# Where the next expert weights are put: ten places of four kinds of tiles instead of five of one kind, and two of four gathers spread over two pairs

## The chip, the cores and the metric

The kernel runs on one core of a Trainium2 chip. The metric is device time in microseconds (us) of one execution; the median of several runs is quoted, and one further execution is recorded by the hardware profiler. Inside a core, TensorE (PE in the rows) multiplies, VectorE (DVE), ScalarE (ACT) and GpSimd (POOL) do the element-wise work, and SyncE (SP) issues most of the copies from device memory. Each engine works through its own list of instructions in order; they wait for each other by semaphores. Copies issued by SP run on 16 DMA engines.

## The reference

The model has two layers of one kind and then two of another, over 512 tokens of width 1024. The change touches only the mixture of experts of the first kind: 16 experts, each with three 1024 x 1024 float32 matrices, and each expert takes the 64 tokens that score highest for it.

```python
def expert_choice_moe(h, w_router, w_gate_e, w_up_e, w_down_e):
    cap = EC_CAPACITY * s // N_EXPERTS                      # 64 tokens
    affinity = jax.nn.softmax((h @ w_router).astype(jnp.float32), axis=-1)
    top_aff, idx = lax.top_k(jnp.swapaxes(affinity, 1, 2), cap)
    xe = h[bidx, idx]
    hid = jax.nn.silu(jnp.einsum('becd,edf->becf', xe, w_gate_e)) * jnp.einsum('becd,edf->becf', xe, w_up_e)
    ye = jnp.einsum('becf,efd->becd', hid, w_down_e)
    return jnp.zeros_like(h).at[bidx, idx].add(ye * top_aff[..., None].astype(ye.dtype))
...
        x = x + expert_choice_moe(rms_norm(x, g_moe[i]), w_router[i], w_exp_gate[i], w_exp_up[i], w_exp_down[i])
        ple_gate = jax.nn.sigmoid(rms_norm(x, g_ple[i]) @ w_ple_gate[i])
        x = x + ple_gate * (p[i] @ w_ple[i])
```

## The kernel before

The experts are worked through in **eight pairs** (`for pr in range(8)` in `moe`). The two experts of a pair use the two halves of the PE's columns (`two[fh][j * 64:...]`, j = 0 and 1), so that a multiplication of the one can run beside a multiplication of the other. A pair is twelve **steps**: four for gate, four for up, four for down. A step uses two **loads** of 1 MB, one of each expert: 2 x 128 rows of 1024 float32 (`take()`), and consists of eight multiplications. So a pair has 24 loads, a layer 192.

`load()` issues the next load on SP's queue and takes its place from a pool of tiles. `plan` says from which:

- `wst`: five tiles of 1 MB (`NW = 5`), which stage all other weights of the kernel too;
- `pt`: three tiles of 1 MB, two of which hold the one-hot matrices `oh` of the slots during the pairs;
- `fm`: tiles of 256 KB, 24 of them; a load takes four, in four copies;
- `wh`: the pair of tiles `wh`, `wl` of 512 KB, two of each; a load takes one of each, in two copies;
- `tr` and `ae`: two more kinds, used once a layer.

A tile that is used again is loaded when the last multiplication that reads its old contents is done; since SP issues in order, a load that waits for its place holds up all later loads. Before, the list `PLAN` uses the further kinds for the first 25 loads of a layer; from there on (`plan.pop(0) if plan else "wst"`) all go to the five `wst` places.

Between the steps of a pair stands other work of the PE, one piece a step, taken from the list `side` by `step()`: the **scatter** of the pair before (`sct`, eight pieces of two multiplications, added to `x` by DVE), `turned` (one-hots of the pair turned, `oht` and `asl`) and, in pairs 1, 3 and 5, the **gather** of the tokens of the next four experts (`xe`, four pieces of 16 multiplications). When `side` is empty, `step()` takes a piece of `late`, the work that prepares the next stage: `turn` (`pps`), eight products `pw` of six multiplications each, whose weights `wple` are loaded and split into `wh`, `wl` first, and the loading (`wpg`) and splitting of the next gate's first weights. Within a pair, the result of gate and up goes through ACT (`sg`), DVE (`hd`), PE (`hdt`) and ACT or DVE (`ht`) before down can begin.

The order on each engine is not that of the program text alone: a scheduler interleaves the instructions, and may put a multiplication of one expert before its partner's weights are expected, as rows below show.

Of the kernel before, what the change touches and what calls it, by code (L numbers as in the profile page):

```python
# [16 lines left out]
S = 512  # L17
D = 1024
KT = 8
NB = 4  # L20
P = 128
# [11 lines left out]
PLAN = ["pt"] * 2 + ["wst"] * 5 + ["fm"] * 3 + ["wh"] * 2 + ["tr", "ae"] + ["pt"] + ["wst"] * 5 + ["fm"] * 3 + ["wh"] * 2  # L33
# [52 lines left out]
class Net:  # L86
# [12 lines left out]
    def claim(self, *tiles):  # L99
        """first touch, so that a tile has its place before those first used from here on"""  # L100
        for t in tiles:
            self.nc.gpsimd.memset(t[:, :1], 0.0)
# [60 lines left out]

    def wtile(self, w, segs, kts):
        """w: AP [K, N]; segs: column ranges; kts: K-tiles -> SBUF view [P, len(kts), cols]"""
# [12 lines left out]
    def wsplit(self, parts, k, m):  # L178
        """parts: list of (dst column 0.., source AP [P, k', m'...]) -> hi, lo [P, k, m]"""
# [23 lines left out]
    def ahead(self, n):  # L203
        """what is traced inside comes up to n instructions earlier in the scheduler's order"""
        return self.tc.high_priority(offset=n) if n else nullcontext()

    def proj_fm(self, w, c0, c1, xh, xl, evac, kn=KT, rope=False, early=0, pre=()):
        """feature-major: out[c, t] for columns c0..c1 (<= 256 a unit); evac(i, m, psum[m, S])"""
# [27 lines left out]
    def proj_tm(self, w, segs, xh, xl, evac):  # L236
        """token-major: out[t, cols] in runs of 256 columns; evac(i, tb, psum[P, 256])"""
# [17 lines left out]
    def split(self, out_h, out_l, src, scale=None):  # L255
        """exact two-part split of src (PSUM or SBUF) into float32r hi, lo"""
# [8 lines left out]

    def inv_rms(self, ms, n):
        """ms: [P, n] SBUF mean square + eps -> ms ** -0.5"""
        r = self.sm("rr", n)
        self.nc.gpsimd.tensor_tensor(r, ms, self.mhalf[:, :n], op=OP.pow)  # L269
        return r  # L270

    def rows(self, r, width=None):
        """r: [P tok, NB] per-token column(s) -> PSUM [P, S], the value of each token on all partitions"""
# [9 lines left out]
    def mean_sq(self, gains=(None,), on=None):  # L283
        """for each gain the mean of (x g)^2 of the residual's tokens, PSUM [P, NB] each"""
# [21 lines left out]
    def rms_cols(self, on=None):  # L306
        """rsqrt(mean(x^2)+eps) of the residual's tokens, [P, NB]"""
# [7 lines left out]
    def norm(self, g, shift=None, before=None):  # L315
        """before: gain of a norm that x has still to go through first (self.r1: its tokens' factors)"""
# [30 lines left out]
    def norm_raw(self, g):  # L347
        """x * g in two parts; the norm's factor of each token is left to the products' ends"""
# [7 lines left out]
    def factors(self, on=None):  # L356
        """the norm's factor of each token: self.rt [P tok, NB] and self.rb [P, S], the same on all partitions"""
# [6 lines left out]
    def fmul(self, out, ps, scale=None, m=P):  # L364
        """feature-major product times the tokens' factors (and a constant)"""
# [5 lines left out]
    def tmul(self, out, ps, tb):  # L371
        """token-major product times the tokens' factors"""
# [7 lines left out]

    def setup(self):
# [7 lines left out]
        # x to feature-major  # L389
# [18 lines left out]
        # vectors, feature-major: column j of vec is row j of the stacked [rows, 128]  # L408
# [30 lines left out]
    def t5_bias(self):  # L439
        """T5 bias vector of each head over the relative position"""  # L440
# [47 lines left out]
    def sgu(self, l, xh, xl, w_in, vv):  # L488
        """spatial gating; vv: gelu(v) token-major tiles (cols 256:512 of each)"""
# [49 lines left out]
    def probs(self, e, s, dst, qb, nk):  # L539
        """normalise e by 1/s [P,1], transpose into dst[:, kt, qb*P:]"""  # L540
# [12 lines left out]
    def gqa(self, l, qkv, av):  # L553
        nc, ap = self.nc, self.ap
        # gains folded into the rope tables, six heads wide
# [83 lines left out]
    def diff_pre(self, l, xh, xl, w_in):  # L639
        nc = self.nc  # L640
        # q and k of a map in exact parts, stacked: (qh qh ql) . (kh kl kh)
# [19 lines left out]
    def diff(self, l, cv, stacked):  # L661
        nc, ap = self.nc, self.ap
        lam_init = 0.8 - 0.6 * math.exp(-0.3 * l)
        # lambda
# [69 lines left out]
    def dt_mul(self, l, w_in):  # L734
        """four partial products of the time steps, on 32 partitions each, from x itself"""
# [15 lines left out]
    def ssm(self, l, xh, xl, w_in, dtv, ahead):  # L751
# [31 lines left out]
        # cumulative sums within each chunk: acs (inclusive towards l) and what is left to the end  # L783
# [11 lines left out]
        # conv + silu, feature-major: x0 x1 b0 b1 c0 c1  # L795
# [17 lines left out]
        # token-major x and b  # L813
# [16 lines left out]
        for g in range(2):  # L830
            # scores [s, (c l)]
# [29 lines left out]
            # inside the chunk  # L861
# [8 lines left out]
            # across chunks: the states before each, [n, (hh p)]  # L870
# [101 lines left out]
    def add_out(self, w, macc, scale, gate=None, fills=(), before=None):  # L972
        """x += gate * ((scale * macc) @ w); before: see norm"""
# [21 lines left out]
    def mix1(self, l, fills):  # L995
        """fills: pieces of work that hang on nothing here"""
# [43 lines left out]
    def moe(self, l, fill, late):  # L1040
        """fill, late: pieces of work that hang on nothing here, for the time of the routing and for after it"""
        nc, ap = self.nc, self.ap
        # the experts' weights in the order of their use, two K-tiles of one expert at a time
# [32 lines left out]
        # the first go wherever there is room during the routing  # L1076
        plan = PLAN[:]
        for _ in range(PLAN.index("tr")):
            load()
        gm = self.vec["g_moe"][:, l * 8:l * 8 + 8]  # L1080
# [5 lines left out]
        # router on x itself; the norm's factor of each token follows on the logits  # L1086
# [34 lines left out]
        # normed x (without its gain) token-major in two exact parts  # L1121
# [19 lines left out]
        # one-hot of the slot of each token in each expert, two tiles of eight experts  # L1141
# [9 lines left out]
        def gather(g4, d2, xs):  # L1151
            # tokens of four experts, feature-major
# [9 lines left out]
            t = self.fm("xe")  # L1162
# [9 lines left out]
        def turned(pr, out):  # L1172
            # slot-major one-hot and affinities of the pair
# [23 lines left out]
        def step():  # L1197
            if side:
                side.pop(0)()
            elif late and pr:  # L1200
                late.pop(0)()
        xs, nxt = [], []
        onehot(0)
        for pr in range(8):
            tn = []
            if pr in (1, 3, 5):
                onehot(pr // 2 + 1)
            side.append(lambda pr=pr, tn=tn: turned(pr, tn))
            if pr % 2 and pr < 7:
# [528 lines left out]
```

## Time and profile before

| | us |
|---|---|
| median of 3 runs (3690.09 to 3692.62) | 3691.54 |
| the profiled execution, span from first to last instruction | 3690.2 |
| eight pairs of the first layer (557.9 to 1131.5) | 573.6 |
| eight pairs of the second layer (1721.4 to 2300.7) | 579.3 |
| mean granted clock of the PE, of full speed | 0.984 |

The profiled execution is reported by its span alone. A row of a stretch gives: its begin and end, its length, and for PE, PEld (the PE's loading of stationary operands), DVE, ACT and POOL the busy time and in brackets the instructions; then the granted clock, the busy share of the DMA engines and the GB/s that they moved. The stretches of the pairs begin at the first expert multiplication of each pair (192 matmul records a pair, two for each multiplication). A row of a timeline gives begin, duration, engine, line, operation, what is written from what, shape and count, and in square brackets how long the engine had been idle before and what ended that. Matmul rows end about 0.07 us after the next one has begun, since matmuls are pipelined.

### The profile page before, as it was taken

The numbers are of one execution on the slowest core, as the hardware profiler recorded it, in microseconds if no ns is written. First come the engines' busy times: TensorE is split into PE (matmuls) and PEld (weight loads), VectorE is DVE, ScalarE is ACT, GpSimd is POOL, SyncE is SP. The second block draws the span as 40 slices with busy tenths as digits, with TensorE's granted clock in tenths as the row PEclk, the third lists the DMA queues.
The fourth block names the chain that finished last, engine by engine and source line by source line (L and its number), as shares of the span: only waits on it lengthen the run. The fifth ranks groups of instructions, "written<-read, shape, count | busy, mean of one in ns | idle before, by whom it ended". The sixth has DMA issues, their size and how long they took to land. (4 is left out here: it accounts for less than half of the span.)

```text
span 3690.2 us, 41806 instructions
## 1 busy us (share of the span) xinstructions
PE 3505.6 (95%) x15959; PEld 2302.9 (62%) x15959; DVE 1804.6 (49%) x3532; ACT 1134.1 (31%) x2209; POOL 416.9 (11%) x630
## 2 busy tenths in 40 slices
PE   8999989999999999999999899899999999999998
PEld 7867774333336877776333333676768877676887
DVE  7667651111106776773111011787564458866344
ACT  4334731000004443462000001424443332444333
POOL 0110620000000110061000000131030003203000
PEclk9999999999999999999999999999999999999999
DMA  5223758888896132565888989222213333220322
GB/s 171 90 69 111 225 203 311 327 330 330 312 358 207 58 106 82 169 224 214 320 329 315 357 311 359 89 77 85 69 35 107 99 107 100 64 81 31 114 96 69
DMA packets 335580, 655.93 MB, mean 178 GB/s; under 512 B 28188, under 2 KB 205680, under 8 KB 335380
## 3 DMA queue, kind: packets, MB, share of 16 engines
q1 hardware_dynamic: 312128, 628.77, 47.8%
q0 software_dynamic: 8192, 15.22, 1.8%
q10 hardware_dynamic: 15059, 9.28, 0.8%
q8 instruction: 126, 2.06, 0.2%
q14 instruction: 75, 0.61, 0.1%
HBM read 629.59 MB, written 14.70 MB: 175 GB/s over the span
## 5 line engine op out<-in xcount | busy, mean ns | idle before, releaser
L150 PE MATMUL pj<-xh,wh 128*128 128x512 f32 x1808 | 729.0, 404 | 15.0 <-DVE gb L147 6.6
L150 PE MATMUL pj<-xh,wl 128*128 128x512 f32 (+1 forms) x1808 | 725.7, 402 | 10.9 <-DVE wl L139 10.9
L150 PE MATMUL pj<-xl,wh 128*128 128x512 f32 (+1 forms) x1808 | 726.0, 402 | 0.9 <-DVE xl L147 0.7
L150 PE MATMUL eg<-wst,xe 128*64 128x512 f32 x1872 | 535.3, 604 | 47.8 <-DMA wst<-in_w_exp_up_dram 40.2
L129 ACT ACTIVATE wh<-wst 128x1024 fp32r<-128x1024 f32 (+2 forms) x368 | 339.0, 930 | 758.1 <-PE pj L150 565.1
L139 DVE TENSOR_TENSOR wl<-wst,wh 128x1024 fp32r<-128x1024 f32 (+2 forms) x368 | 412.2, 1123 | 310.9 <-ACT wh L129 310.4
L150 PEld LDWEIGHTS pj<-xh,wh 128*128 128x128 f32 x1808 | 342.8, 190 | 110.8 <-DVE gb L147 9.8
L150 PEld LDWEIGHTS pj<-xh,wl 128*128 128x128 f32 (+1 forms) x1808 | 342.6, 190 | 103.3 <-DVE wl L139 14.2
L150 PEld LDWEIGHTS pj<-xl,wh 128*128 128x128 f32 (+1 forms) x1808 | 342.5, 189 | 94.1 <-issue 12.8
L150 PEld LDWEIGHTS eg<-wst,xe 128*64 128x64 f32 x1872 | 167.7, 136 | 367.8 <-issue 249.2
L150 PE MATMUL ey<-wst,ht 128*64 128x512 f32 x960 | 298.7, 602 | 14.4 <-DVE ht L136 6.3
L139 DVE TENSOR_TENSOR hd<-sg,eg 128x512 f32<-128x512 f32 x32 | 21.9, 685 | 451.9 <-PE eg L150 422.9
L150 PEld LDWEIGHTS ey<-wst,ht 128*64 128x64 f32 x960 | 87.3, 136 | 161.2 <-issue 132.8
L269 POOL TENSOR_TENSOR rr<-msb,mhalf 128x4 f32<-128x4 f32 x9 | 9.2, 1021 | 1518.8 <-DVE msb L143 1518.8
L150 PE MATMUL pt<-wh,xh 128*128 128x256 f32 x512 | 145.8, 285 | 1.5 <-DVE ro L139 1.2
L150 PE MATMUL pt<-wl,xh 128*128 128x256 f32 x512 | 144.7, 283 | 0.0
L150 PE MATMUL pt<-wh,xl 128*128 128x256 f32 x512 | 144.7, 283 | 0.0
L139 DVE TENSOR_TENSOR x<-x,sct 128x512 f32<-128x512 f32 x128 | 82.3, 682 | 118.6 <-PE sct L150 118.6
L129 ACT ACTIVATE e<-e,nm 128x512 f32<-128x512 f32 (+3 forms) x192 | 111.2, 581 | 69.7 <-DVE nm L143 69.2
L129 ACT ACTIVATE sg<-eg 128x512 f32<-128x512 f32 x32 | 19.1, 596 | 323.1 <-PE eg L150 323.1
L1364 POOL TENSOR_TENSOR wada<-wada 128x1024 f32<-128x1024 f32 (+1 forms) x48 | 101.8, 2121 | 133.0 <-ACT wada L129 131.2
L134 ACT ACTIVATE ht<-hdt 128x512 f32<-128x512 f32 x16 | 9.6, 597 | 342.6 <-PE hdt L154 342.6
(485 smaller groups left out, 5380.7 us busy)
## 6 DMA issues: line engine op xcount, KB each, us to landing
wst<-in_w_exp_gate_dram SPq DMA_DIRECT2D x120, 1024.0 KB, 5.0
wst<-in_w_exp_down_dram SPq DMA_DIRECT2D x120, 1024.0 KB, 7.4
wst<-in_w_exp_up_dram SPq DMA_DIRECT2D x114, 1024.0 KB, 7.4
wst<-in_w_in_dram SPq DMA_DIRECT2D x90, 1024.0 KB, 5.4
wst<-in_w_branch_gate_dram SPq DMA_DIRECT2D x32, 1024.0 KB, 5.8
wada<-in_w_ada_dram SPq DMA_DIRECT2D x24, 1024.0 KB, 5.3
wst<-in_w_out_dram SPq DMA_DIRECT2D x16, 1024.0 KB, 7.7
xd<-x SPq DMA_DIRECT2D x32, 256.0 KB, 2.1
```

Source lines behind the costliest of these rows:

```text
L129: return self.nc.scalar.activation(out, in_, func, **kw)
L134: self.nc.scalar.activation(out, in_, AF.Copy)
L139: return self.nc.vector.tensor_tensor(out, a, b, op=op)
L150: return self.nc.tensor.matmul(out, lhsT, rhs, start=start, stop=stop, **kw)
L269: self.nc.gpsimd.tensor_tensor(r, ms, self.mhalf[:, :n], op=OP.pow)
L1364: nc.gpsimd.tensor_tensor(t[:, :k], t[:, :k], t[:, k:2 * k], op=OP.add)
```

## The change

`PLAN` is replaced by a list `FIRST` of 11 loads for the time of the routing (12 before), followed by one each in `tr` and `ae` as before, and then a `RING` of ten places, repeated until 144 loads, those of pairs 0 to 5, are planned: one `pt`, five `wst`, two of four `fm` tiles, two `wh`/`wl`. The loads of pairs 6 and 7 go to `wst` alone. The gathered tokens no longer take new `fm` tiles in each gather, but two fixed sets of four (`xes`), claimed by eight small writes on POOL. `GATHER` says which pair does which pieces: group 1 wholly in pair 1 as before, group 2 half in pair 2 and half in pair 3 (before: pair 3), group 3 half in pair 4 and half in pair 5 (before: pair 5). The pieces of `late` come only from pair 6 on, and then one a step beside a piece of `side` (`if late and pr >= 6` instead of `elif late and pr`).

```diff
-PLAN = ["pt"] * 2 + ["wst"] * 5 + ["fm"] * 3 + ["wh"] * 2 + ["tr", "ae"] + ["pt"] + ["wst"] * 5 + ["fm"] * 3 + ["wh"] * 2
+FIRST = ["pt"] * 2 + ["wst"] * 5 + ["fm"] * 2 + ["wh"] * 2
+RING = ["pt"] + ["wst"] * 5 + ["fm"] * 2 + ["wh"] * 2
+GATHER = {1: (1, (0, 1, 2, 3)), 2: (2, (0, 1)), 3: (2, (2, 3)), 4: (3, (0, 1)), 5: (3, (2, 3))}
...
-        plan = PLAN[:]
-        for _ in range(PLAN.index("tr")):
+        plan = FIRST + ["tr", "ae"]
+        while len(plan) < 6 * 24:
+            plan += RING
+        plan = plan[:6 * 24]
+        for _ in FIRST:
             load()
+        xes = [[self.fm("xe") for _ in range(4)] for _ in range(2)]
+        self.claim(*xes[0], *xes[1])
...
-            t = self.fm("xe")
+            t = xes[g4 % 2][d2]
...
             if side:
                 side.pop(0)()
-            elif late and pr:
+            if late and pr >= 6:
                 late.pop(0)()
...
-            if pr in (1, 3, 5):
-                onehot(pr // 2 + 1)
-            side.append(lambda pr=pr, tn=tn: turned(pr, tn))
-            if pr % 2 and pr < 7:
+            g4, part = GATHER.get(pr, (0, ()))
+            if part and part[0] == 0:
+                onehot(g4)
                 nxt = []
-                for d2 in range(4):
-                    side.append(lambda g4=pr // 2 + 1, d2=d2, nx=nxt: gather(g4, d2, nx))
+            side.append(lambda pr=pr, tn=tn: turned(pr, tn))
+            for d2 in part:
+                side.append(lambda g4=g4, d2=d2, nx=nxt: gather(g4, d2, nx))
```

**SP, the loads of pairs 1 and 2.** Each row is a copy into the tile named first, with its shape and how many stand in a row; `we` are the tiles of the further kinds. Before:

```order
L1069 DMA wst<-in_w_exp_gate_dram 128x2x1024 x7
L1069 DMA wst<-in_w_exp_up_dram 128x2x1024 x8
L1069 DMA wst<-in_w_exp_down_dram 128x2x1024 x8
L1069 DMA wst<-in_w_exp_gate_dram 128x2x1024 x8
L1069 DMA wst<-in_w_exp_up_dram 128x2x1024 x8
```

Now, from the first gate loads of pair 1 on:

```order
L1071 DMA wst<-in_w_exp_gate_dram 128x2x1024 x5
L1059 DMA we<-in_w_exp_gate_dram 128x512 x8
L1064 DMA wewh<-in_w_exp_gate_dram 128x1024
L1064 DMA wewl<-in_w_exp_gate_dram 128x1024
L1064 DMA wewh<-in_w_exp_up_dram 128x1024
L1064 DMA wewl<-in_w_exp_up_dram 128x1024
L1071 DMA we<-in_w_exp_up_dram 128x2x1024
L1071 DMA wst<-in_w_exp_up_dram 128x2x1024 x5
```

Ten loads that were ten copies of 1 MB are now six of 1 MB, eight of 256 KB and four of 512 KB. In the program each of these loads waits for the step that used the load ten before it; before, for the step that used the load five before it.

**ACT, pairs 2 and 3.** ACT evacuates half of each gather piece (`xe`) and each product (`pw`), so its list shows in which pair they stand; `yh` begins the scatter of the pair. Before:

```order
L129 ACTIVATE oht<-oht 128x512
L129 ACTIVATE ph_5718<-pps 128x512
L129 ACTIVATE ph_5727<-pps 128x512
L129 ACTIVATE pw_5761<-pw 128x512
L129 ACTIVATE pw_5782<-pw 128x512
L129 ACTIVATE yh<-ey_5677,asl 128x512
L129 ACTIVATE yh<-ey_5678,asl 128x512
L129 ACTIVATE sg<-eg_5796 128x512
L134 ACTIVATE ht<-hdt 128x512
L129 ACTIVATE sg<-eg_5797 128x512
L129 ACTIVATE oht<-oht 128x512
L129 ACTIVATE xe<-xe,vec_158 128x256 x4
```

Now:

```order
L131 ACTIVATE oht<-oht 128x512
L131 ACTIVATE xe<-xe,vec_158 128x256 x2
L131 ACTIVATE yh<-ey_5741,asl 128x512
L131 ACTIVATE yh<-ey_5742,asl 128x512
L131 ACTIVATE sg<-eg_5866 128x512
L136 ACTIVATE ht<-hdt 128x512
L131 ACTIVATE sg<-eg_5867 128x512
L131 ACTIVATE oht<-oht 128x512
L131 ACTIVATE xe<-xe,vec_158 128x256 x2
```

The four pieces of gather 2 stood in pair 3 and now stand two and two; the work on `pps` and `pw` has left pair 2.

**PE, the beginning of pair 6.** `eg` are the expert multiplications of gate, written for one half of the result each. Before:

```order
L150 MATMUL eg_6672<-wst,xe 64x512
L150 MATMUL eg_6673<-wst,xe 64x512
L150 MATMUL sct<-oht,yh 128x512
L150 MATMUL sct<-oht,yl 128x512
L150 MATMUL sct<-oht,yh 128x512
L150 MATMUL sct<-oht,yl 128x512
L150 MATMUL sct<-oht,yh 128x512
L150 MATMUL eg_6672<-wst,xe 64x512
L150 MATMUL eg_6673<-wst,xe 64x512
L150 MATMUL eg_6672<-wst,xe 64x512 x2
L150 MATMUL eg_6673<-wst,xe 64x512 x2
```

Now, from its third step on:

```order
L152 MATMUL pw<-ph_6797,wh 128x512
L152 MATMUL pw<-pl_6798,wh 128x512
L152 MATMUL sct<-oht,yh 128x512
L152 MATMUL sct<-oht,yl 128x512
L152 MATMUL pw<-ph_6797,wl 128x512
L152 MATMUL pw<-ph_6806,wh 128x512
L152 MATMUL pw<-pl_6807,wh 128x512
L152 MATMUL pw<-ph_6806,wl 128x512
L152 MATMUL eg_6779<-wst,xe 64x512
L152 MATMUL eg_6780<-wst,xe 64x512
```

All eight products `pw` stand in pair 6 now (before: two in pair 2, three each in pairs 4 and 6). In both kernels, two multiplications of the same step often stand alone ahead of another piece, as the first two rows of before: they read the weights of one expert, and their partners come after the piece.

## Rows read from the trace of the kernel before

**Rows 1.** The page: span and busy time of the PE.
```profile
span 3690.2 us, 41806 instructions
...
PE 3505.6 (95%) x15959; PEld 2302.9 (62%) x15959; DVE 1804.6 (49%) x3532; ACT 1134.1 (31%) x2209; POOL 416.9 (11%) x630
```
**Rows 2.** Stretches: pairs 0 to 7 of layer 0, in columns as above.
```profile
557.90:610.00 52.10, 51.39 (x256) 26.02 (x258) 6.51 (x16) 6.34 (x11) 0.00 (x0) 1.00 0.88 331
610.00:685.10 75.10, 73.08 (x299) 29.97 (x295) 14.55 (x23) 7.86 (x13) 0.00 (x0) 1.00 0.81 304
685.10:756.60 71.50, 66.74 (x249) 25.06 (x248) 10.15 (x18) 5.93 (x10) 0.00 (x0) 1.00 0.87 338
756.60:836.10 79.50, 74.50 (x294) 30.41 (x293) 10.94 (x20) 5.56 (x10) 0.00 (x0) 1.00 0.86 330
836.10:909.00 72.90, 67.83 (x248) 25.28 (x247) 8.94 (x16) 5.45 (x9) 0.00 (x0) 1.00 0.85 332
909.00:989.70 80.70, 74.71 (x294) 30.45 (x293) 10.83 (x20) 5.55 (x10) 0.00 (x0) 1.00 0.84 325
989.70:1062.80 73.10, 67.34 (x247) 25.41 (x246) 8.89 (x16) 5.45 (x9) 0.31 (x1) 0.98 0.86 331
1062.80:1131.50 68.70, 61.14 (x226) 21.65 (x225) 10.10 (x17) 4.97 (x7) 0.00 (x0) 1.00 0.98 375
sum 573.60, PE 536.73 PEld 214.25 DVE 80.90 ACT 47.11 POOL 0.31; mean PE 67.09 PEld 26.78 DVE 10.11 ACT 5.89 POOL 0.04
```
**Rows 3.** Stretches: the sum over the eight pairs of layer 1.
```profile
sum 579.30, PE 538.30 PEld 213.23 DVE 80.25 ACT 48.02 POOL 0.00; mean PE 67.29 PEld 26.65 DVE 10.03 ACT 6.00 POOL 0.00
```
**Rows 4.** SP's queue, pairs of layer 0: waited for what, total us, times, longest.
```profile
SPq L1069 <- PE eg L150: 298.8, 110, 11.4
SPq L1069 <- PE ey L150: 176.6, 46, 8.0
```
**Rows 5.** Short stretches inside pairs 3 and 6 of layer 0, same columns.
```profile
776.60:804.60 28.00, 24.78 (x92) 8.34 (x88) 1.62 (x3) 1.68 (x3) 0.00 (x0) 1.00 1.03 411
993.70:997.70 4.00, 4.00 (x14) 1.42 (x13) 0.03 (x1) 0.00 (x0) 0.00 (x0) 1.00 0.27 68
```
**Rows 6.** Timeline of the PE in pair 2 of layer 0.
```profile
704.64 4.49 PE L150 MATMUL eg<-wst,xe 128*64 128x512 f32 x16 [0.52 <-DMA wst<-in_w_exp_gate_dram]
...
734.90 3.65 PE L150 MATMUL ey<-wst,ht 128*64 128x512 f32 x12
738.48 1.09 PE L154 MATMUL pps<-ident,pin 128*128 128x128 f32 x8
739.50 1.93 PE L150 MATMUL ey<-wst,ht 128*64 128x512 f32 x4
```
**Rows 7.** Timeline of the PE in pair 0: first and last of 20 gather rows.
```profile
562.62 0.28 PE L150 MATMUL xe<-oh,h2l 128*128 128x256 f32 x1
...
564.89 0.28 PE L150 MATMUL xe<-oh,h2l 128*128 128x256 f32 x1
```
**Rows 8.** Stretch of pair 4, instructions of the scatter alone: PE busy.
```profile
836.10:909.00 72.90, 5.56 (x17) 1.00 0.85 332
```
**Rows 9.** Stretch of pair 4, instructions of the products `pw` alone: PE busy.
```profile
836.10:909.00 72.90, 4.99 (x18) 1.00 0.85 332
```
**Rows 10.** Timeline of SP in pair 0: twelve copies of 256 KB.
```profile
580.66 8.07 SPq L1057 DMA_DIRECT2D we<-in_w_exp_down_dram  x12
```
**Rows 11.** Short stretch in pair 0 while these move, same columns.
```profile
583.00:592.00 9.00, 9.00 (x45) 5.75 (x42) 0.00 (x0) 0.00 (x0) 0.00 (x0) 1.00 1.03 383
```
**Rows 12.** The page: the splits into `wh` and `wl`, mean ns after the comma.
```profile
L129 ACT ACTIVATE wh<-wst 128x1024 fp32r<-128x1024 f32 (+2 forms) x368 | 339.0, 930 | 758.1 <-PE pj L150 565.1
L139 DVE TENSOR_TENSOR wl<-wst,wh 128x1024 fp32r<-128x1024 f32 (+2 forms) x368 | 412.2, 1123 | 310.9 <-ACT wh L129 310.4
```
**Rows 13.** Timeline of POOL ahead of the pairs of layer 0.
```profile
479.21 0.31 POOL L1084 MEMSET wrz<- 128x256 f32 x1 [9.26 <-DVE macc L139]
532.25 1.02 POOL L269 TENSOR_TENSOR rr<-msb,mhalf 128x4 f32<-128x4 f32 x1 [52.73 <-DVE msb L143]
```

More of the change, by code (lines that the diff above doesn't have):

```diff
@@ L1205, in moe @@
             tn = []
-            if pr in (1, 3, 5):
-                onehot(pr // 2 + 1)
+            g4, part = GATHER.get(pr, (0, ()))
+            if part and part[0] == 0:
+                onehot(g4)
+                nxt = []
             side.append(lambda pr=pr, tn=tn: turned(pr, tn))
-            if pr % 2 and pr < 7:
-                nxt = []
-                for d2 in range(4):
-                    side.append(lambda g4=pr // 2 + 1, d2=d2, nx=nxt: gather(g4, d2, nx))
+            for d2 in part:
+                side.append(lambda g4=g4, d2=d2, nx=nxt: gather(g4, d2, nx))
             xc = pr % 2 * P
```

## The prediction

> **What bounds the kernel now.** I read first the page: the PE is busy 95% of the span [rows 1], which would leave little to gain from loading earlier. So the next view is that of the stretches, pair by pair [rows 2]. The reader is to see that the pairs of one kind of work do not take what that work takes: pairs 2, 4 and 6 take 71.5 to 73.1 us, pairs 3 and 5 some 80, and the load rate is the same in both, 325 to 338 GB/s. A pair loads 24 x 1,048,576 bytes = 25.2 MB. Inside the pairs the rate is not steady: 411 GB/s over 28 us of pair 3, but 68 GB/s over 4 us of pair 6 [rows 5]. The timeline shows both sides [rows 6]: where the PE has only expert work, sixteen records take 4.49 us and 0.52 us of idle time before them, ended by a load, so loads set the pace there; where scatter, gather or products stand between the steps, the PE takes longer than the loads, the five places are full, and SP waits for the PE (475 of 574 us in all [rows 4], most of it harmless queueing, but the 68 GB/s are there). So neither side is the bound throughout. They take turns, because five places, two of them being read, hold only about three loads ahead.
>
> How much is lost by that follows from what each side needs. **Loads:** at 411 GB/s one load takes 2.55 us and a pair 61.2 us. **PE:** I call two expert multiplications side by side a slot. Rows 6 give the price: four records (two slots when the partners stand apart) 1.93 us, twelve (four slots) 3.65 us; so 0.86 us a slot, and about 0.15 us for each unbroken run of them after taking off the 0.07 us under the next row (738.48 against 734.90 + 3.65). A perfect pair is 48 slots. Counted in the order of the PE, with partners apart where another piece comes between, the pairs 0 to 7 of before have 49, 58, 56, 60, 56, 60, 56, 54 slots in 6, 14, 9, 12, 9, 12, 9, 6 runs (layer 0; layer 1 has one run and at most two slots more in a pair). Other work: pair 0 takes 52.10 us [rows 2], its slots 43.0 us, its 48 gather multiplications 48 x 0.1135 us ((564.89 - 562.62) / 20 [rows 7]) = 5.4 us, which leaves 3.7 us for the turning of gate and up and its waits. A later pair adds the scatter, 5.6 us [rows 8], and about 1 us for the turned one-hots (one piece like `pps` [rows 6]): 10.3 us. A whole gather is 64 x 0.1135 = 7.3 us. So pair 3 needs 60 x 0.86 + 12 x 0.15 + 10.3 + 7.3 = 71.0 us and took 79.5; pair 4 needs 49.5 + 10.3 + 5.0 (products [rows 9]) = 64.8 and took 72.9; pair 7 needs 56 and took 68.7. Some 8 us a pair are lost, 12 in pair 7.
>
> **The change, part by part.** *Ten places.* With them a load waits for the step that used the load ten before, so about eight loads, 8 x 2.55 = 20 us, stand ahead of the PE. A scatter of 5.6 us, a half gather of 3.6 us or the turning then costs the loads nothing, and a stretch of pure expert work lives on the stock. What is late next is whichever side needs more over a whole pair. Loads: two of ten places are filled by 256 KB copies. For these rows 10 and 11 are the nearest: while twelve of them are issued, the rate is 383 GB/s, so such a load takes 2.74 us and a pair 19.2 x 2.55 + 4.8 x 2.74 = 62.1 us. Bounds: 61.2 (no difference) and 76.0 (25.2 MB at the 331 GB/s that pair 0 shows as a whole [rows 2], which holds waits for places too). I take 62.1, since rows 11 are the same kind of copy.
>
> On this price the Trainium skill speaks against the change. Its page "DMA: Bandwidth & Descriptors" (Where 436 GB/s comes from) says that the HBM side binds a core's loads at about 358 GB/s; an estimate by that page of the Trainium skill is 70.3 us a pair, and with five loads of stock used up 266.6 us for pairs 2 to 5, 3611 us in all. The trace does not agree: it holds 411 GB/s for 28 us [rows 5], so the sum does not use it.
>
> PE, after: the slots are 49, 58, 54, 57, 56, 56, 60, 54 in 6, 14, 9, 10, 10, 9, 14, 6 runs. The two half gathers are 3.6 us in each of pairs 2 to 5.
> - Pair 0: no loads were awaited there before (52.1 us against a need built on itself); stays 52.1.
> - Pair 1: 49.9 + 2.1 + 10.3 + 7.3 = 69.6 (took 75.1).
> - Pairs 2 to 5: 47.8, 50.5, 49.7, 49.5 us of slots and runs, each + 10.3 + 3.6: 61.7, 64.4, 63.6, 63.4, in all 253.1. Loads need 4 x 62.1 = 248, less the stock. So the PE is the bound by about 1 us a pair, and 253.1 stand against 304.6 before.
> - Pair 6: 51.6 + 2.1 + 10.3, eight products at 4.99 / 3 = 1.66 us each = 13.3, and `pps` 1.1: 78.4 us against 73.1. This is the price of moving all products into one pair: 5.3 us lost. Loads (24 and the two of the next stage, 66 us) hide under it, though the ring is back to five places.
> - Pair 7: bound by loads as before, less one load (`wpg`, now in pair 6): 68.7 - 2.6 = 66.1.
>
> Sum 519.3 us against 573.6, so 54.3 us less in layer 0; with the same work and one run more a pair 520 against 579.3 [rows 3], 59 less in layer 1. In all 113 us.
>
> *Edits at nothing.* The eight claims stand on POOL ahead of `rr`, which needs the residual complete; they wait for the last multiplications of the stage before, and POOL is idle 52.73 us there until the mean square arrives [rows 13]. Uncovered they would cost at most 8 x 0.31 = 2.5 us a layer (the longer write of rows 13). One load less ahead of the routing: pair 0 runs at the pace of the PE with 14 loads before it, and with 13 the next are issued as its first steps end; at worst one load, 2.6 us. The load `wple` now sits in SP's queue at the start of pair 6, and its two splits wait for the `wh`, `wl` that pair 5 reads last; they take 2 x (0.93 + 1.12) = 4.1 us [rows 12], while two steps and two scatter pieces, 8 us, stand before the first product. Uncovered: up to 4 us a layer.
>
> *Unknown.* Short waits between two sides that need nearly the same: between 0 and 1.5 us in each of the twelve pairs 1 to 6; I take 0.5, 6 us in all. Then 3690.2 - 113 + 6 = 3583 us, and the median stands 1.3 us above the profiled span: **3584 us**.
>
> **Rivals.**
> 1. *The loads become the bound*, because many small copies do not keep 411 GB/s. For it: the ring has eighteen copies for ten loads, and pair 0, the only stretch with such copies, shows 331 GB/s. Against: rows 11. At 331 GB/s pairs 2 to 5 take 4 x 76 less five loads of stock of 3.2 us = 288 us, 35 more a layer: 3654 us. Any rate between gives a time between this and the forecast.
> 2. *The PE is the bound already*, and the change buys only its fewer slots. For it: 95% busy [rows 1]. Against: sixteen records at 4.49 us beside twelve at 3.65, with idle time ended by a load [rows 6]; a busy PE is partly a waiting one. Slots: 449 to 444 a layer, so 2 x 5 x 0.86 = 9 us: 3683 us.
> 3. *Slower: the small copies hold up SP's queue.* If the twelve small copies of a round take t each, one after the other, a round of ten loads takes 6 x 2.55 + 12t us, and the 91 loads of pairs 2 to 5 beyond the stock take 9.1 rounds. From t = 1.5 us on they take the 304.6 us of before, and the other pairs give back only 2.8 us. With t = 2 it is 357 us, 50 more a layer: about 3790. For it: order alone, since every later load stands behind them. Against: twelve were issued in 8.07 us [rows 10], 0.67 each, and the data kept pace [rows 11]. The same page of the Trainium skill (Anatomy of one DMA) gives a copy issued on GpSimd's queue some 2 us of fixed time; an estimate from that is 2.6 us for 256 KB by itself. No run here shows a small copy of SP by itself, and those of rows 10 and 11 overlap.
>
> **How the numbers follow.** Forecast, 3560 to 3602 us: 0.72. Rival 1, 3602 to 3660: 0.14. Rival 2, near the old time: 0.07, of which 0.03 within 0.2%. Rival 3: 0.05. Below 3560: 0.02. A change under 0.2% (7.4 us) can't be told from none. So faster 0.92, same 0.03, slower 0.05. The range goes from 3560, the sum without residual waits (6 us) and with pair 7 bound by its 24 loads less a stock of two (9 us a layer), up to 3632, halfway into rival 1; it leaves out about 0.2.
>
> **What would show it.** In the changed profile: pairs 2 to 5 at 61 to 66 us each with the load rate near 400 GB/s as a mean; hardly any 16-record row of 4.49 us in them; pair 6 near 78 us and longer than its neighbours; pair 7 unchanged in kind. SP should wait for steps that lie five back. The forecast is wrong if the expert rows of pairs 2 to 5 still end waits for a load (rival 1, with the rate of these stretches as its measure), if pairs 2 to 5 lose their DMA pauses and still take 72 to 80 us (rival 2), or if pair 6 takes much over 80, from products waiting for `wple`.

## The result, and the profile after

The changed kernel takes **3592.06 us** (median of 4 runs, 3591.32 to 3597.67), the kernel before 3690.82 beside it: a ratio of 0.9736, 95% interval 0.9722 to 0.9750, or 98.8 us less. Forecast were 3584 us, in a range of 3560 to 3632. The page has these rows, the last two of the groups of instructions that read `wst`:

```profile
span 3589.6 us, 42088 instructions
...
PE 3442.5 (96%) x15959; PEld 2290.9 (64%) x15959; DVE 1805.2 (50%) x3532; ACT 1133.4 (32%) x2209; POOL 418.0 (12%) x646
...
L152 PE MATMUL eg<-wst,xe 128*64 128x512 f32 x1264 | 362.5, 598 | 8.3 <-DMA wst<-in_w_exp_up_dram 6.4
...
L152 PE MATMUL ey<-wst,ht 128*64 128x512 f32 x624 | 197.8, 601 | 14.4 <-DMA wst<-in_w_exp_down_dram 5.6
```

The busy share of the PE says as little as in [rows 1]: 96% for 95%. The stretches say it, cut at the first expert multiplication of each pair as in [rows 2, 3]; first pairs 0 to 7 of layer 0, then the sum of layer 1, then four short pieces, of pairs 6, 7, 7 and 3:

```profile
558.50:610.60 52.10, 51.41 (x257) 26.02 (x258) 3.84 (x8) 5.49 (x10) 0.00 (x0) 1.00 0.88 331
610.60:682.20 71.60, 70.20 (x298) 29.21 (x294) 15.13 (x29) 6.79 (x12) 0.00 (x0) 1.00 0.99 388
682.20:743.70 61.50, 59.39 (x259) 25.15 (x258) 9.38 (x17) 4.50 (x8) 0.00 (x0) 1.00 1.02 387
743.70:809.10 65.40, 63.54 (x263) 26.02 (x262) 10.63 (x19) 4.60 (x8) 0.00 (x0) 1.00 0.98 383
809.10:872.40 63.30, 61.54 (x260) 24.94 (x259) 9.40 (x17) 4.43 (x8) 0.00 (x0) 1.00 1.03 402
872.40:936.40 64.00, 62.10 (x265) 26.02 (x264) 10.33 (x19) 5.00 (x10) 0.00 (x0) 1.00 0.98 384
936.40:1016.70 80.30, 78.15 (x284) 31.34 (x283) 15.48 (x22) 13.19 (x20) 0.31 (x1) 1.00 0.78 297
1016.70:1084.40 67.70, 60.09 (x226) 21.49 (x225) 7.65 (x15) 2.97 (x5) 0.00 (x0) 1.00 0.93 355
sum 525.90, PE 506.44 PEld 210.19 DVE 81.84 ACT 46.96 POOL 0.31; mean PE 63.30 PEld 26.27 DVE 10.23 ACT 5.87 POOL 0.04
...
sum 528.30, PE 506.88 PEld 209.59 DVE 81.01 ACT 47.59 POOL 0.00; mean PE 63.36 PEld 26.20 DVE 10.13 ACT 5.95 POOL 0.00
...
936.40:943.40 7.00, 7.00 (x31) 2.88 (x31) 4.06 (x6) 2.87 (x4) 0.00 (x0) 1.00 0.09 9
1016.70:1032.70 16.00, 15.28 (x53) 5.71 (x53) 5.13 (x9) 0.00 (x0) 0.00 (x0) 1.00 0.78 285
1068.00:1072.00 4.00, 4.00 (x22) 1.61 (x20) 0.00 (x0) 0.00 (x0) 0.00 (x0) 1.00 0.41 102
775.00:779.00 4.00, 4.00 (x22) 1.71 (x20) 0.00 (x0) 0.00 (x0) 0.00 (x0) 1.00 1.05 389
```

Layer 0 gives back 47.7 us, layer 1 51.0, and all else 1.9 (2537.3 us outside the pairs before, 2535.4 now). Pairs 2 to 5 take 254.2 us for 304.6, at 383 to 402 GB/s instead of 325 to 338. The sign that the prediction named for its rival 1 is absent: in these four pairs the PE waits for no load any more. Here are its waits for loads in pairs 2 to 5 of layer 0 before, and all its waits there now (waited for what, total us, times, longest):

```profile
PE eg L150 <- DMA wst<-in_w_exp_up_dram: 10.9, 16, 1.4
PE eg L150 <- DMA wst<-in_w_exp_gate_dram: 2.8, 4, 0.9
...
PE sct L152 <- DVE x L141: 3.0, 8, 0.5
PE ey L152 <- ACT ht L136: 2.7, 4, 0.7
PE asl L152 <- DVE ht L138: 1.0, 3, 0.3
PE sct L152 <- ACT yh L131: 0.8, 1, 0.8
```

Pairs 6 and 7 are the exception: pair 6 is 7.2 us longer than before and pair 7 only 1.0 shorter. The timeline of the PE in pair 7 shows why that pair gains so little, with the very rows that showed the taking of turns in [rows 6]:

```profile
1028.57 7.14 PE L152 MATMUL eg<-wst,xe 128*64 128x512 f32 x32
1036.27 4.49 PE L152 MATMUL eg<-wst,xe 128*64 128x512 f32 x16 [0.57 <-DMA wst<-in_w_exp_gate_dram]
1041.38 4.50 PE L152 MATMUL eg<-wst,xe 128*64 128x512 f32 x16 [0.62 <-DMA wst<-in_w_exp_up_dram]
1047.91 4.49 PE L152 MATMUL eg<-wst,xe 128*64 128x512 f32 x16 [2.03 <-DMA wst<-in_w_exp_up_dram]
```

The 32 records of the first row, from stock, take 7.14 us, 3.57 for sixteen; then each sixteen waits for its load and takes 4.49 or 4.50.

### The profile page after: what moved, and what is told of

Read it like the earlier page. It is cut to its first block, busy times and chain, and to the rows that moved or that the text cites. A ratio compares the mean times of both kernels' runs of the same rounds, so it can differ in the third digit from the quotient of the medians.

```text
span 3589.6 us, 42088 instructions
## 1 busy us (share of the span) xinstructions
PE 3442.5 (96%) x15959; PEld 2290.9 (64%) x15959; DVE 1805.2 (50%) x3532; ACT 1133.4 (32%) x2209; POOL 418.0 (12%) x646
## 5 line engine op out<-in xcount | busy, mean ns | idle before, releaser
L152 PEld LDWEIGHTS pj<-xh,wl 128*128 128x128 f32 (+1 forms) x1808 | 342.2, 189 | 102.7 <-DVE wl L141 13.7
L152 PE MATMUL eg<-wst,xe 128*64 128x512 f32 x1264 | 362.5, 598 | 8.3 <-DMA wst<-in_w_exp_up_dram 6.4
L152 PEld LDWEIGHTS eg<-wst,xe 128*64 128x64 f32 x1264 | 116.9, 136 | 193.3 <-issue 167.3
L152 PE MATMUL ey<-wst,ht 128*64 128x512 f32 x624 | 197.8, 601 | 14.4 <-DMA wst<-in_w_exp_down_dram 5.6
L152 PE MATMUL eg<-we,xe 128*64 128x512 f32 x496 | 199.3, 596 | 0.1
L152 PEld LDWEIGHTS ey<-wst,ht 128*64 128x64 f32 x624 | 58.0, 136 | 109.4 <-issue 81.8
L152 PE MATMUL ey<-we,ht 128*64 128x512 f32 x240 | 108.1, 598 | 1.5 <-DVE ht L138 0.8
```

The lines of the kernel that those rows point to most:

```text
L152: return self.nc.tensor.matmul(out, lhsT, rhs, start=start, stop=stop, **kw)
```

## The experiments

Times are medians, ratios those to the kernel before, with 95% intervals. "Pairs 2 to 5" is their sum in layer 0 (changed kernel: 254.2 us). My theory is that of the prediction: five places let the two sides take turns, ten let each pair take what its slower side needs. Its rivals were a bound by the loads (1), a PE that was the bound already (2), and small copies that hold up SP's queue (3).

**The ring taken out** (`e1`), **gathers whole again** (`e2`), **seven places** (`e7`), **nine and four places** (`e12`). The first two split the change in its parts, the others change one size.

```diff
# e1
-        while len(plan) < 6 * 24:
-            plan += RING
-        plan = plan[:6 * 24]
+        plan += RING
# e2
-GATHER = {1: (1, (0, 1, 2, 3)), 2: (2, (0, 1)), 3: (2, (2, 3)), 4: (3, (0, 1)), 5: (3, (2, 3))}
+GATHER = {1: (1, (0, 1, 2, 3)), 3: (2, (0, 1, 2, 3)), 5: (3, (0, 1, 2, 3))}
# e7
-RING = ["pt"] + ["wst"] * 5 + ["fm"] * 2 + ["wh"] * 2
+RING = ["wst"] * 5 + ["fm"] * 2
# e12
-NW = 5
+NW = 4
-FIRST = ["pt"] * 2 + ["wst"] * 5 + ["fm"] * 2 + ["wh"] * 2
-RING = ["pt"] + ["wst"] * 5 + ["fm"] * 2 + ["wh"] * 2
+FIRST = ["pt"] * 2 + ["wst"] * 4 + ["fm"] * 2 + ["wh"] * 2
+RING = ["pt"] + ["wst"] * 4 + ["fm"] * 2 + ["wh"] * 2
```

Expected of `e1`: 

> The ring of ten places is taken out of the change: after the first loads of a layer all go to the five wst places again, while the spread gathers and the products in pair 6 stay. My theory: the two sides take turns because five places hold only about three loads ahead. Then pairs 2 to 5 fall back from 61 to 65 us to about 73 to 76 each (the old gather pairs took 80 with a whole gather of 7.3 us, the others 72 with none or products; a half gather lies between), the waits of the expert rows for loads come back, and the time is 3680 to 3700 us, most of the gain gone. Rival (the PE was the bound already, and only its slots count): the slots are nearly those of the changed kernel (447 against 444 in a layer), so the time stays at 3590 to 3600 us. Rival (the gain came from the spread of the gathers): half or more of the gain stays, 3640 us or less.

Expected of `e2`: 

> The ring stays, and the gathers of groups three and four stand whole in pairs 3 and 5 again. My theory: with some eight loads ahead of the PE the two sides need to agree over several pairs only, so it matters little where a gather stands. By the sum, pairs 3 and 5 need 52.4 and 51.4 us of slots and runs, 10.3 and a whole gather of 7.3, that is 70.0 and 69.0; pairs 2 and 4 need 55.8 and 57.6 on the PE, less than the loads' 62.1, so they are bound by loads, unless the stock covers it: the pair after a gather begins with a full ring of ten, some 20 us of stock, while only 4 to 6 us are lacking. Four pairs: between 252 us (stock covers all) and 263 us (no stock), against 254 measured in the changed kernel. So 3588 to 3612 us, and within 0.2% of the changed kernel at the low end. Rival (the spread of the gathers is what won the time): pairs 3 and 5 go back to 78 to 80 us, pairs 2 and 4 stay at 62 or above: 3640 us or more.

Expected of `e7`: 

> From pair 1 on a ring of seven places (five wst, two of four fm) instead of ten; pairs 6 and 7 as in the changed kernel. Theory of turns: what counts is how long the loads can go on while the PE does other work. Seven places, two of them being read, leave about five loads, 13 us. In pairs 2 to 5 a scatter of 5.6 us, a half gather of 3.6 and the turning stand in some 30 us of a pair between expert steps, and the two sides need the same within 1 us, so part of the stock's work is undone: pairs 2 to 5 take 63 to 68 us, between the 71.6 of five places and the 63.5 of ten, nearer to ten: 3595 to 3625 us in all. Rival (any more places than five already give all): 3590 to 3595. Rival (it is the kinds of tiles, each with its own turn, not the number of places): 3650 or more.

Expected of `e12`: 

> One wst tile less in the whole kernel: nine places in the ring instead of ten, and four instead of five in pairs 6 and 7 and in all other stages. Theory of turns: nine places are still about seven loads ahead, so pairs 2 to 5 stay within 1 us of the changed kernel each (254 us for four), while pairs 6 and 7, which live on wst alone, lose as much again as five places lose there, 3.6 and 12.1 us in layer 0: 84 and 80 us instead of 80.2 and 67.7. Other stages may lose too, that is read apart. Rival (pairs 6 and 7 are over the sum for another reason, the rate of the loads or waits for products): they stay within 2 us of 80 and 68 each.

| | us | ratio | pairs 2 to 5 | pairs 6, 7 |
|---|---|---|---|---|
| `e1`, five places | 3677.31 | 0.9967 (0.9955 to 0.9979) | 286.4 | 81.0, 67.3 |
| `e7`, seven | 3619.06 | 0.9807 (0.9794 to 0.9821) | 262.1 | 82.1, 67.5 |
| `e12`, nine; four in pairs 6, 7 | 3636.42 | 0.9853 (0.9839 to 0.9866) | 253.9 | 85.2, 72.6 |
| changed kernel, ten | 3592.06 | 0.9736 (0.9722 to 0.9750) | 254.2 | 80.3, 67.7 |
| `e2`, ten, gathers whole | 3587.99 | 0.9725 (0.9710 to 0.9739) | 252.9 | 80.3, 67.5 |

The stretches of pairs 2 to 5 of `e2`, and their sum:

```profile
682.20:736.40 54.20, 52.85 (x228) 21.38 (x227) 11.28 (x23) 3.51 (x6) 0.00 (x0) 1.00 1.01 383
736.40:808.30 71.90, 69.77 (x295) 29.82 (x294) 11.57 (x21) 5.70 (x11) 0.00 (x0) 1.00 1.03 404
808.30:865.00 56.70, 54.94 (x228) 21.23 (x227) 8.46 (x15) 3.48 (x6) 0.00 (x0) 1.00 1.00 388
865.00:935.10 70.10, 68.21 (x297) 30.04 (x296) 11.28 (x21) 5.93 (x12) 0.00 (x0) 1.00 0.98 387
sum 252.90, PE 245.76 PEld 102.47 DVE 42.59 ACT 18.61 POOL 0.00; mean PE 61.44 PEld 25.62 DVE 10.65 ACT 4.65 POOL 0.00
```

Rival 2 is out: `e1` has the slots of the changed kernel within three a layer, and all but 13 us of the gain is gone (it came out even a little faster than I had put: 71.3 to 72.3 us a pair for 73 to 76, and 3677 us for at least 3680). The PE's waits for loads in its pairs 2 to 5 are back, 14.1 us in 20 waits, for 13.7 in 20 before the change. The time follows the places: 286.4, 262.1, 253.9 and 254.2 us with five, seven, nine and ten, and the sum's need of the PE was 253.1. `e2` is the plainest picture of a stock: pairs 2 and 4 take 54.2 and 56.7 us, less than any 24 loads can be moved in, because what they lack was put aside in pairs 1 and 3. With ten places the spread of the gathers is worth nothing (the intervals of `e2` and of the changed kernel overlap); with five, pairs 2 to 5 fell by 18 us, from 304.6 to 286.4. How much of that is the spread is not shown, since five of the products left these pairs too; and pairs 1 and 6 of `e1` lose most of it again (79.0 and 81.0 for 75.1 and 73.1). In `e12` pairs 6 and 7 lose 4.9 us each (I had written 4 and 12: right in kind, and too much for pair 7), and the other stages 30 us, which is no matter of this change.

**The loads by themselves** (`e5`). Left out are the scatter and the gathers of groups 2 to 4.

```diff
-                nxt = []
...
-            for d2 in part:
-                side.append(lambda g4=g4, d2=d2, nx=nxt: gather(g4, d2, nx))
...
-                for d in range(4):
-                    side.append(lambda i=dh * 4 + d, yh=yh, yl=yl, oht=tn[0]: scatter(i, yh, yl, oht))
...
-            if pr % 2:
-                xs = nxt
```

> To let the loads alone set the pace of pairs 1 to 5, the scatter of the experts' results and the gathers of groups two to four are left out (the experts' results are not added, and all pairs read the tokens of group one). The PE then needs about 43.5 us of slots and runs and 5 us of other work in each of these pairs, 49 us, far below the loads. My theory: the loads of the mixed ring move at 383 to 411 GB/s as a mean, so pairs 2 to 5 take 61 to 63 us each, nearly what they take in the changed kernel with all its side work, and the rate of these stretches is about 400 GB/s. Rival 1 (many small copies do not keep the rate): 331 GB/s and 76 us a pair, so that these pairs would become longer than with the side work, which can only be if the side work hid nothing. The rate of the page weighed in the prediction, about 358 GB/s, would give 70 us. What the measured pair says is also how near the changed kernel already is to the loads' own limit: at 62 us nothing more is to be had in pairs 2 to 5 beyond 1 to 3 us each.

Measured: 3520.81 us, and these stretches of pairs 2 to 5:

```profile
663.90:725.00 61.10, 53.30 (x215) 18.92 (x212) 3.89 (x7) 3.65 (x7) 0.00 (x0) 1.00 1.03 404
725.00:788.40 63.40, 54.75 (x214) 19.02 (x212) 3.88 (x7) 3.62 (x7) 0.00 (x0) 1.00 1.03 405
788.40:848.70 60.30, 52.51 (x214) 18.65 (x212) 3.88 (x7) 3.67 (x7) 0.00 (x0) 1.00 1.03 403
848.70:913.20 64.50, 55.95 (x223) 20.76 (x220) 5.17 (x9) 5.17 (x9) 0.00 (x0) 0.97 1.03 405
sum 249.30, PE 216.51 PEld 77.35 DVE 16.82 ACT 16.11 POOL 0.00; mean PE 54.13 PEld 19.34 DVE 4.21 ACT 4.03 POOL 0.00
```

The DMA share is 1.03 throughout, and a pair of loads is 62.3 us long; I had put 62.1. Rival 1 with its 331 GB/s is out. The rate of the Trainium skill's page "DMA: Bandwidth & Descriptors" (Where 436 GB/s comes from), about 358 GB/s on the HBM side, which it works out as half of what two cores share, did not bind this one core either: here 403 to 405 were moved for 249 us. And the changed kernel, at 254.2, is within 5 us of the loads alone, and within about 1 of the sum's need of the PE, 253.1: further places have next to nothing left to bring in pairs 2 to 5.

**Twice the copies**: in `fm` (`e3`), in `wh` and `wl` by rows (`e9`) and by columns (`e10`).

```diff
# e3
-                        nc.sync.dma_start(t[k * 2 + h], src[:, k, h * S:h * S + S])
+                        for r in (slice(0, 64), slice(64, P)):
+                            nc.sync.dma_start(t[k * 2 + h][r], src[r, k, h * S:h * S + S])
# e9
-                    nc.sync.dma_start(t[k], src[:, k])
+                    for r in (slice(0, 64), slice(64, P)):
+                        nc.sync.dma_start(t[k][r], src[r, k])
# e10
-                    nc.sync.dma_start(t[k], src[:, k])
+                    for h in range(2):
+                        nc.sync.dma_start(t[k][:, h * S:h * S + S], src[:, k, h * S:h * S + S])
```

Expected of `e3`: 

> Each copy of 256 KB is issued as two copies of 128 KB (64 rows each), so that ten loads of the ring are 26 copies instead of 18, and 16 of them are smaller still. My theory (small copies in flight cost little, about the 383 GB/s of the rows in pair 0, and SP issues one in far less time than it moves): pairs 2 to 5 stay at 61 to 65 us, the time within 0.3% of the changed kernel, 3588 to 3603 us. Rival (each small copy has a price t that adds up in the queue, with t above 0.7 us): eight more copies in ten loads add 8 x 0.7 = 5.6 us to a round of ten loads, 13 us to a pair of 24: loads would need 75 us a pair and the time would rise by 80 us or more. In between: if the loads need 2 us more a pair they pass the PE's 63 and pairs 2 to 5 show waits for loads, some 10 us in all.

It took 3695.83 us (1.0012, 1.0003 to 1.0021), pairs 2 to 5 303.7: the whole gain lost, 104 us, against my expectation and as the rival in it had said (80 us or more). But the edit had changed two things, the number of copies and the rows that each fills. Hence the next two.

Expected of `e9`: 

> Each 512 KB copy into wh or wl is issued as two copies of 64 rows and 256 KB, so that ten loads of the ring are 22 copies instead of 18. The run with copies of 128 KB lost the whole gain, against my expectation. What its trace shows: eight such copies behind each other were issued 0.6 us apart and moved 194 to 218 GB/s, and each copy waits for the copy eight before it. Theory A (a copy costs SP's queue about 0.6 us whatever it carries, so that 128 KB cannot keep 411 GB/s and 256 KB, 0.64 us at that rate, just can): this kernel keeps the rate, and its time is within 0.3% of the changed kernel, 3585 to 3603. Theory B (copies of 64 rows are slow as such, at about half the rate): the eight copies of 256 KB for two loads take 1.2 us each, some 5 us more for ten loads and 11 us more a pair, and the time goes to 3660 us or more. Theory C (each further copy adds about 0.6 us): four more in ten loads add 2.4 us, 6 us a pair, of which some 5 show beside a PE need 1 us above the loads': about 3630.

Expected of `e10`: 

> As the run by rows, but each 512 KB copy is issued as two copies of 128 rows and half the columns, 256 KB each in rows of 2 KB, the form of the fm copies. Theory A (0.6 us a copy, whatever it carries): within 0.3% of the changed kernel, 3585 to 3603. Theory B (64 rows are slow as such): the same here, 3585 to 3603, since all 128 rows are used, while the run by rows is slow. Theory C (each further copy adds): about 3630, as by rows.

`e9` took 3693.30 us (1.0007, 0.9990 to 1.0023; pairs 2 to 5 304.0), `e10` 3589.79 (0.9727, 0.9715 to 0.9740; 252.9). The same number of copies, the same 256 KB in each: theories A and C are out, and it is the 64 rows. In ten loads `e9` moves as many bytes by copies over 64 rows as `e3`, 2 MB, and loses as much, so nothing is left for `e3`'s copies being smaller; copies of 128 KB over all rows were not tried. A stretch of `e9` while such copies move:

```profile
710.00:718.00 8.00, 4.51 (x16) 1.10 (x12) 0.00 (x0) 0.00 (x0) 0.00 (x0) 0.93 1.01 235
```

The engines count as busy all the time (1.01) and move 235 GB/s; with copies of 256 KB over all rows it was 389 (the last piece of the stretches after). The Trainium skill's page "SBUF — State Buffer" (Door 1: The DMA port swizzle) says it: rows 0 to 63 are reached through 8 of 16 ports, and it gives 196 GB/s for them, measured at 1 MB; the 235 here are above that and far below 389. The same page of the Trainium skill, in its section on whether two DMAs can hit both halves, says that the two serialize; here, where copies of the lower and the upper rows take turns in the queue, 235 is far from twice 196. So my first reading of `e3` in theory A, 0.6 us a copy whatever it carries, was wrong, and rival 3 has nothing left that speaks for it: four more copies in ten loads, each over all rows, cost nothing (all eight pairs of layer 0 took 525.8 us in `e10` and 525.9 in the changed kernel).

**Pairs 6 and 7.** Seven places there too (`e6`), the same with the products spread (`e8`), the products alone spread (`e4`), and two `pt` tiles in pair 7 (`e13`).

```diff
# e6 and e8, behind plan = plan[:6 * 24]
+        while len(plan) < 8 * 24:
+            plan += (["wst"] * 5 + ["fm"] * 2)
+        plan = plan[:8 * 24]
# e4 and e8; turn = [0] ahead of step()
         def step():
+            turn[0] ^= 1
...
-            if late and pr >= 6:
+            if late and pr >= 6 and turn[0]:
# e13, behind plan = plan[:6 * 24]
+        plan += (["wst"] * 26 + (["pt"] * 2 + ["wst"] * 5) * 4)[:48]
```

Expected of `e6`: 

> The loads of pairs 6 and 7 go to seven places (five wst, two of four fm tiles) instead of the five wst. In the changed kernel pair 6 took 80.2 us, 1.8 over the sum, and pair 7 67.7, 1.6 over it; its expert runs there hold 3.6 and 12.1 us more than their slots and runs cost. My theory: what the two pairs lose is the return to five places, first because the first loads of pair 6 find all five wst in use (almost nothing moves for the first 7 us of it), then because a stock of three loads does not outlast the products and the scatter. With seven places pair 6 takes the sum's 78 us or a little less, and pair 7 comes near the 62 us of its loads, or below by what is in stock: together 138 to 143 us instead of 147.9, 5 to 10 us a layer, 3572 to 3583 us. Rival (pair 7 is bound by the rate of its loads as such): only the wait in pair 6 goes, 2 to 4 us a layer, 3585 to 3589. Rival (pair 6 is long because products wait for the splits of wple): no change in pair 6 at all.

Expected of `e8`: 

> Seven places in pairs 6 and 7 as in the run beside it, and the products no longer all in pair 6: a piece of late comes only at every other step, so that five stand in pair 6 and three in pair 7. The work of the PE over both pairs is nearly the same (112 slots in 19 runs became 111 in 23), so by the theory that both pairs together are bound by the PE once the loads have enough places, this gains nothing over seven places alone: within 4 us of that run, 3570 to 3583. Rival (five places were the lesser trouble, the heaping of products in pair 6 the greater): it is faster than seven places alone by 6 us or more.

Both got slower than the changed kernel by some 35 us: 3627.47 (0.9830, 0.9817 to 0.9842) and 3628.41 (0.9830, 0.9818 to 0.9843), pairs 6 and 7 168.7 and 167.6 us instead of 148.0. SP's queue in pair 6 of `e6`:

```profile
957.98 0.51 SPq L1071 DMA_DIRECT2D wst<-in_w_exp_up_dram  x1
975.10 0.80 SPq L1059 DMA_DIRECT2D we<-in_w_exp_up_dram  x2
975.96 0.42 SPq L1071 DMA_DIRECT2D wst<-in_w_exp_up_dram  x1
```

For 16.6 us nothing is issued. In the program the copy at 975.10, the last quarter of a load, waits for a tile that is read in the step that this load itself feeds (the wait ends with a multiplication of gate and up, `eg`), and copies further on wait for the products' multiplications or for `ph`. I had not counted the `fm` tiles: of 24, `x` holds 8, the tokens 4, `ph` and `pl` 4 and `pw` one after another 8, so from pair 6 on there are no two loads' worth of them. A place that is lent out to other work is none, and in a queue in order it stops those behind it too. The edit thus said nothing on my theory.

Expected of `e4`: 

> The loads stand as in the changed kernel (wst alone from pair 6 on); only the products move: a piece of late comes at every other step, five products in pair 6 and three in pair 7. By the sum pair 6 needs 51.4 us of slots and runs, 10.3, five products of 1.66 and 1.1, that is 71.1 on the PE, pair 7 47.5, some 9 for scatter and one-hots and 5.0, that is 61.5, against loads of 61 to 62. With five places a pair whose sides need nearly the same lost about 8 us before, and 3.6 when the PE needed far more: 75 to 79 and 67 to 70, together 142 to 148 against 147.9 in the changed kernel. So 3580 to 3593 us. Rival (heaping the products costs nothing in itself, since the loads hide under them, and spreading only makes both pairs suffer from five places): together 150 or more, 3596 and up.

It took 3593.23 us (0.9740, 0.9724 to 0.9756): no gain. Pairs 6 and 7 went from 80.3 and 67.7 to 74.9 and 77.3 in layer 0, from 80.4 and 68.0 to 74.7 and 74.1 in layer 1. Together they take 152.2 and 148.8 us, where I had put 142 to 148 and the rival 150 or more, against 148.0 and 148.4 in the changed kernel. So the products took their time with them into pair 7, and with five places spreading them gained nothing.

Expected of `e13`: 

> In pair 7 two pt tiles join the five wst places, from its third load on; they come free when the last splits of pair 6 are done, some 10 us before pair 6 ends, so that no load waits for another stage's work (which is what went wrong with the fm tiles, held by ph, pl and pw). Theory: what pair 7 loses is stock; in the changed kernel its loads pause some 5 us in all during its first scatter pieces (about 280 GB/s over the first 16 us) and 3 us near its end, and then 28 slots run at the pace of the loads. With two more loads in stock at its begin (5.1 us) and seven places, pair 7 takes 62 to 64 us instead of 67.7, pair 6 stays at 80: 3.5 to 6 us less a layer, 3580 to 3585 us. Rival (pair 7 is bound by the rate of the loads from its first step to its last, whatever the places): 67 to 68 us and no change, 3590 to 3594. Rival (the two loads taken in early hold up the wst loads behind them): pair 6 grows by some us and eats the gain.

It took **3579.57 us** (0.9686, 0.9668 to 0.9704), 12.5 us under the changed kernel and the fastest of all that leave no work out. Pairs 6 and 7 of layer 0, pair 7 of layer 1:

```profile
933.40:1013.70 80.30, 78.14 (x283) 31.27 (x282) 15.35 (x22) 13.15 (x20) 0.31 (x1) 1.00 0.79 296
1013.70:1074.40 60.70, 56.97 (x226) 21.44 (x225) 7.67 (x15) 2.97 (x5) 0.00 (x0) 1.00 1.03 401
2124.20:2185.20 61.00, 57.49 (x226) 21.33 (x225) 7.64 (x15) 3.08 (x5) 0.00 (x0) 1.00 1.03 401
```

Pair 7 goes from 67.7 to 60.7 us, more than I had expected, at a DMA share of 1.03: now it is the rate of its loads that binds it. The pauses of the changed kernel's pair 7, 16 us at 285 GB/s and 4 at 102, are (411 - 285) / 411 x 16 + (411 - 102) / 411 x 4 = 7.9 us of loads not moved, near the 7.0 that came back.

## Why the prediction was right, and where its sum was off

*What bounds the kernel.* Right: that the sides took turns, shown by `e1`, `e7` and `e12`, where little but the number of places changes in pairs 2 to 5, by `e2`, and by the waits for loads, which are gone there.

*Loads, 62.1 us a pair; pairs 2 to 5, 253.1 us.* Right: 62.3 by `e5`, and 254.2 measured (255.8 in layer 1). The four pairs came to 61.5, 65.4, 63.3 and 64.0 for 61.7, 64.4, 63.6 and 63.4. The mixed places cost at most 1.1 us a pair by `e5` (62.3 for 61.2), where the sum had put 0.9.

*Edits at nothing.* They cost nothing that shows: pair 0 has 52.1 us as before, and outside the pairs the time fell by 1.9 us.

*Residual waits, 0.5 us in each of twelve pairs.* Too small, though they can't be told from the errors of the other terms. Layer 0 is 6.6 us over the sum without waits, where 3 were allowed. Of the twelve pairs, the two pairs 1 are over most, by 2.0 and 2.3 us, then the two pairs 6, by 1.9 and 2.0, the others by at most 1.2.

*Pair 6, 78.4 us: "the loads hide under it".* The price of all products was right in size; the cover was too thin. The ring leaves a stock, but the queue then stands for 7 us (9 GB/s) because the next loads want `wst` tiles that are still in use, and with five places the end of the pair ran dry. In its last twelve slots, which cost 10.4 us by the prices of [rows 6], the PE spent 14.0:

```profile
1001.24 9.76 PE L152 MATMUL ey<-wst,ht 128*64 128x512 f32 x36
1011.64 3.65 PE L152 MATMUL ey<-wst,ht 128*64 128x512 f32 x12 [0.63 <-DMA wst<-in_w_exp_down_dram]
```

Measured were 80.3, so 1.9 us were missing in this term; the rest of the pair took some 1.7 us less than its terms.

*Pair 7, 66.1 us: "bound by loads as before, less one load".* This is the step that failed in its reason. It took 67.7, and the load that left bought 1.0 us instead of 2.6. Pair 7 was not bound by the number of its loads but by the pauses between them, which `e13` took away. That the `wpg` load had partly stood in time that was lost anyway would explain the missing 1.6 us, but no run shows it.

Sum: 6.6 us more in layer 0 and 8.3 in layer 1 than the sum without waits, less the 6 allowed and the 1.9 outside, are the nearly 7 us between the forecast's span of 3583 and 3589.6.

## What to carry to other kernels

Where a queue of loads and an engine each wait for the other in the same stage, work out what each needs over a whole period: the time is the larger of the two plus what the stock is too small for, and places are worth adding only until it covers the longest stretch without their work. Count places by who else takes the tiles of that kind in that stage, since one lent tile stops all loads behind it. When copies are split, split them so that each still covers all 128 rows.

## What the hardware showed that I had not expected

Copies over 64 rows moved 235 GB/s, copies of the same 256 KB over 128 rows 389, with the DMA engines counted busy in both. And a long wait for loads is followed by a slower PE: in pair 7 of `e6` it was busy 3.83 of 8 us, and in the next 8 us the granted clock was 0.61 of 2.4 GHz, mostly the lower level of 1.2. Records right behind the wait of 4.26 us last 1.06 to 1.11 us; those of 11 us later, in a stretch at 1.00, last 0.59:

```profile
1034.00:1042.00 8.00, 3.83 (x14) 0.99 (x12) 2.50 (x4) 0.00 (x0) 0.00 (x0) 0.97 0.86 283
1042.00:1050.00 8.00, 7.30 (x22) 2.57 (x24) 0.00 (x0) 0.00 (x0) 0.00 (x0) 0.61 1.03 411
1050.00:1058.00 8.00, 7.85 (x34) 2.70 (x30) 0.00 (x0) 0.60 (x1) 0.00 (x0) 1.00 0.44 147
...
1042.70 1.11 PE L152 MATMUL eg<-we,xe 128*64 128x512 f32 x1 [4.26 <-DMA we<-in_w_exp_gate_dram]
1043.61 1.06 PE L152 MATMUL eg<-we,xe 128*64 128x512 f32 x1
...
1054.09 0.59 PE L152 MATMUL eg<-we,xe 128*64 128x512 f32 x1
```

How much time this cost the kernel is not shown: in the slow stretch the loads moved at 411 GB/s, so they may have set the pace there too.
